# One decoder layer, two token halves in the MLP: accumulators opened by a copy, the scaled residual added later

## The chip, the cores and the metric

The kernel runs on one core of a Trainium2 chip. A core has a matrix engine (TensorE, PE in the profile), three engines for elementwise work (VectorE or DVE, ScalarE or ACT, GpSimd or POOL) and SyncE (SP), which here does nothing but issue transfers. Each engine runs its own instructions in order and waits on semaphores for the others. The metric is device time in microseconds, as the median of several executions. Tables and rows of the profile are from one further execution, recorded by the hardware profiler.

## The reference, cut to what matters

One decoder layer is computed for 2048 prompt tokens and for 32 decode tokens (8 sequences of 4). The first part (modulated input, a Mamba-2 group beside sliding-window attention, output projection, first layer norm) is not touched. The change lies in what follows:

```python
x = layer_norm(ALPHA * x + g_m * mixed, ln1_g, ln1_b)
h = x * (1.0 + sc_f) + sh_f
u = jnp.square(jax.nn.relu(jnp.einsum('btd,df->btf', h, w_up)))     # 1024 -> 4096
f = jnp.einsum('btf,fd->btd', u, w_down)                            # 4096 -> 1024
x = layer_norm(ALPHA * x + g_f * f, ln2_g, ln2_b)
```

The sum `ALPHA * x + g_f * f` is the subject. The kernel keeps the normalised but not yet scaled x of the prompt in DRAM as `xhat1_d`, so `ALPHA * x` is `xhat * ag1 + ab1`, with `ag1 = ALPHA * ln1_g` and `ab1 = ALPHA * ln1_b` as rows repeated over the partitions. The factor g_f is folded into the down-projection weights (`gf`).

## The kernel before, in words

The MLP is lines 1191 to 1494. It runs in two halves of eight tiles of 128 tokens. Half 1 has two column groups of 512 tokens in its up-projection, half 2 three of 352, since its last group also carries the 32 decode tokens.

The 4096 hidden features are 32 blocks of 128, called f. `up(f)` (L1242) makes one block for all tokens of the half: a group is 8 x 3 matmuls into a bank of PSUM named `sc`. There are three because each fp32 operand is split into a high and a low part (L161 to L168; weights `wuh`/`wul`, `wvh`/`wvl`, `wdh`/`wdl`). ACT then rectifies the group (L1254) and squares it into the high part (L1256), DVE squares it exactly (L1260) and POOL subtracts the two to get the low part (L1261). The pairs of high and low parts are named `x`/`ulx`, `u`/`B` and `A`/`ho` in turn. `ud` (L1259) is the decode tokens' part.

`down` (L1270) takes two blocks f and f+1 at a time: for each tile and each half of the 1024 columns six matmuls of 128x512 into a rotating bank (five of them: three named `mm`, two named `tr` in half 1 and `sc` in half 2), and then DVE adds the bank to the tile's accumulator (L1287). The accumulators are eight tiles of 128x1024 named `p`. In half 2 there are decode matmuls ahead of each (L1275). Sixteen pairs of blocks make up a half; one pair has two `up` and one `down`.

Weights come by SyncE's queue (L1128, 512 KB each) into one of three buffers `st`. Down-projection weights are scaled by DVE (L1137). ACT takes the high part of each (L162), POOL the low part (L163).

The accumulators begin as the scaled residual. `acc_load(t)` (L1224) loads xhat of a tile straight into `p` (L1226), `acc_init(t)` (L1228) multiplies by `ag1` and adds `ab1` in place (L1230, L1231, both DVE). For half 1 the loads are issued ahead of `up(1)` (L1406 to L1411). The initialisations go in a list `bg`, from which `slot()` (L1235) runs one entry after every group of an `up` and every tile of a `down`. For half 2 the entries of `bg` are filled at L1449: entry k has the layer norm of tile k of half 1 (`finish`: statistics L1320 and L1294, L173, L174, L1299 to a scale and shift, ACT L1303, DVE L1306, POOL L1307), the store of the tile before on ACT's queue (L1314), the load of half 2's accumulator two behind and its initialisation three behind. They run beside the last `down` of half 1 and the first `up` of half 2.

Program order is not the final order. A scheduler places each engine's instructions by its own model of their times, subject to what depends on what, so an edit in one place can move instructions in another.

Of the kernel before, what the change touches and what calls it, by code (L numbers as in the profile page):

```python
# [13 lines left out]
AF = mybir.ActivationFunctionType  # L14
ALU = mybir.AluOpType
# [104 lines left out]
def body(tc, I, O):  # L120
    nc = tc.nc
    V, S, G, PE, D = nc.vector, nc.scalar, nc.gpsimd, nc.tensor, nc.sync
# [3 lines left out]
    def pool(name, **kw):  # L126
        return tc.alloc_tile_pool(name=name, bufs=1, reuse_waits="tile", **kw)
# [3 lines left out]
    def mm_tile():  # L131
        return ps.tile([128, 512], F32, tag="mm", name="mm", bufs=3)

    def tr_tile():
        return ps.tile([128, 512], F32, tag="tr", name="tr", bufs=2)

    def sc_tile():
        return ps.tile([128, 512], F32, tag="sc", name="sc", bufs=3)

    xhat1_d = tc.dram_tile([NTOK, DM], F32, name="xhat1_d")  # L140
# [24 lines left out]
    def mm3(out, ahi, alo, bhi, blo, first=True, last=True):  # L165
        PE.matmul(out, lhsT=ahi, rhs=bhi, start=first, stop=False)  # L166
        PE.matmul(out, lhsT=ahi, rhs=blo, start=False, stop=False)  # L167
        PE.matmul(out, lhsT=alo, rhs=bhi, start=False, stop=last)  # L168
# [584 lines left out]
    for i in range(n + 3):  # L753
# [3 lines left out]
        t = g(i)  # L757
# [216 lines left out]
    def prt(i, dt_=F32):  # L974
        return pr.tile([128, 1024], dt_, tag=f"p{i}", name=f"p{i}")
# [47 lines left out]
    def ada_row(r, j, P):  # L1023
        if P == 128:
            return bcast(r, ada_d[0, 1024 * j:1024 * j + 1024])
        D.dma_start(out=r[:ND], in_=ada_d[1:9, 1024 * j:1024 * j + 1024].unsqueeze(1).to_broadcast([NB, NT_, 1024]))
        return r
# [98 lines left out]
    def wraw(nm, f, st=None):  # L1126
        st = st or t4("st")
        D.dma_start(out=st, in_=I["wu"][f].rearrange("p k n -> p (k n)") if nm == "wu" else I["wd"][f])  # L1128
        pre[nm, f] = st
# [11 lines left out]
    def wu_pq():  # L1141
        return [pq.tile([128, 1024], F32R, tag="wu" + c, name="wu" + c) for c in "hl"]
# [52 lines left out]
    def q4(tag):  # L1195
        nb, ty = T4[tag]
        return p4.tile([128, 512 if tag == "r" else 1024], ty, tag=tag, name=tag, bufs=nb)
# [3 lines left out]
    def t4(tag):  # L1201
        return f4.pop(tag) if tag in f4 else q4(tag)

    gf = t4("gf")
    fr = {nm: p4.tile([128, 1024], F32, tag=nm, name=nm) for nm in ("ag1", "ab1", "g2", "b2")}
# [10 lines left out]
    acc = {}  # L1216

    def rows_in():
        for nm, j in (("ag1", 2), ("ab1", 3)):
            bcast(fr[nm], I["rows"][j])  # L1220
        S.activation(fr["ag1"], fr["ag1"], AF.Copy, scale=ALPHA)
        S.activation(fr["ab1"], fr["ab1"], AF.Copy, scale=ALPHA)

    def acc_load(t):  # L1224
        a = acc[t] = prt((2, 3, 7, 4, 1, 5, 6, 0)[t % 8])
        D.dma_start(out=a, in_=xhat1_d[128 * t:128 * t + 128])  # L1226

    def acc_init(t):  # L1228
        a = acc[t]
        V.tensor_tensor(a, a, fr["ag1"], ALU.mult)  # L1230
        V.tensor_tensor(a, a, fr["ab1"], ALU.add)  # L1231

    bg = []

    def slot():  # L1235
        for fn in bg.pop(0) if bg else ():
            fn()

    def wup(f, eng=None):
        wu[f] = wtile("wu", f, *(wu_pq() if f % 2 == 0 else (t4("wvh"), t4("wvl"))), eng=eng)  # L1240

    def up(f, groups, H, u=None):  # L1242
        if f not in wu:
            wup(f)
        wh, wl, _ = wu.pop(f)
        uh, ul = u or u_pair()
        ud = None
        for j, (o, n) in enumerate(groups):
            mm = sc_tile()
            for k in range(8):  # L1250
                ks = slice(128 * k, 128 * k + 128)
                mm3(mm[:, :n], wh[:, ks], wl[:, ks], H[j][0][:, k, :n], H[j][1][:, k, :n], k == 0, k == 7)
            r = t4("r")
            S.activation(r[:, :n], mm[:, :n], AF.Relu)  # L1254
            w = min(n, 1024 - o)
            S.activation(uh[:, o:o + w], r[:, :w], AF.Square)  # L1256
            if w < n:
                ud = p4.tile([128, 32], F32, tag="ud", name="ud", bufs=4)
                V.tensor_tensor(ud, r[:, w:n], r[:, w:n], ALU.mult)  # L1259
            V.tensor_tensor(r[:, :w], r[:, :w], r[:, :w], ALU.mult)  # L1260
            G.tensor_tensor(ul[:, o:o + w], r[:, :w], uh[:, o:o + w].bitcast(F32), ALU.subtract)  # L1261
            slot()
        return uh, ul, ud
# [3 lines left out]
    def wdown(f):  # L1267
        return wtile("wd", f, t4("wdh"), t4("wdl"), gf)

    def down(us, ws, f0, t0, dec, after=None):  # L1270
        if dec is not None:
            for i, w in enumerate(ws):
                for n in range(2):
                    q = 32 * (2 * ((f0 + i) % 2) + n)
                    PE.matmul(dec[q:q + 32, :], lhsT=us[i][2], rhs=w[2][:, 512 * n:512 * n + 512],  # L1275
                              start=f0 + i < 2, stop=f0 + i >= 30, tile_position=(0, q))
        for j in range(8):
            t = t0 + j
            o = 128 * j
            for n in range(2):  # L1280
                sl = slice(512 * n, 512 * n + 512)
                mm = mm_tile() if dnc[0] % 5 < 3 else tr_tile() if dec is None else sc_tile()
                dnc[0] += 1
                for i, w in enumerate(ws):
                    mm3(mm, us[i][0][:, o:o + 128], us[i][1][:, o:o + 128], w[0][:, sl], w[1][:, sl], i == 0,
                        i == len(ws) - 1)
                V.tensor_tensor(acc[t][:, sl], mm, acc[t][:, sl], ALU.add)  # L1287
                if after:
                    after(j, n)
            slot()  # L1290
# [100 lines left out]
    for half in range(2):  # L1391
        t0 = 8 * half
        if half:
            groups, H = [(0, 352), (352, 352), (704, 352)], H3
            dec = tr_tile()
        else:
            groups, H = [(0, 512), (512, 512)], H2
        us, ws = {}, {}
        us[0] = up(0, groups, H)
        if not half:  # L1400
            wup(1, V)
            ada_row(gf, 5, 128)
        ws[0] = wdown(0)
        ws[1] = wdown(1)
        if not half:
            for j in range(2):  # L1406
                acc_load(j)
            rows_in()
            wraw("wu", 2)
            for j in range(2, 8):  # L1410
                acc_load(j)  # L1411
            ds = dec_steps()
            for j in range(8):
                bg.append([lambda j=j: acc_init(j)])
        us[1] = up(1, groups, H)
        for fb in range(15):
            f = 2 * fb
            us[f + 2] = up(f + 2, groups, H)
            if fb:
                ws[f] = wdown(f)  # L1420
                ws[f + 1] = wdown(f + 1)
            if half and fb == 14:
                ul31 = wu_pq()
                us[31] = up(31, groups, H, ul31)
                break
            down([us.pop(f), us.pop(f + 1)], [ws.pop(f), ws.pop(f + 1)], f, t0, dec)
            us[f + 3] = up(f + 3, groups, H)
            next(ds, None)
        if half:
            break  # L1430
        ph.release()
        ph = pool("h2b", side="right")
        H3 = [[ph.tile([128, 8, 352], F32R, name=f"H3_{j}{i}") for i in range(2)] for j in range(3)]
        ws[30] = wdown(30)
        ws[31] = wdown(31)
        wup(0)
        for j in range(3):
            for i in range(2):
                a = 352 * j
                while a < 352 * (j + 1):  # L1440
                    e = min((a // 128 + 1) * 128, 352 * (j + 1))
                    D.dma_start(out=H3[j][i][:, :, a - 352 * j:e - 352 * j].bitcast(F32),
                                in_=h2_d[a // 128][:, i, :, a % 128:a % 128 + e - a])
                    a = e
        wup(1)
        wraw("wd", 0)
        wraw("wd", 1)
        wraw("wu", 2)
        for sl_ in range(12):  # L1449
            todo = []  # L1450
            for lag, fn in ((0, lambda j: finish(j)), (1, lambda j: y_store(j, acc[j], 128, S)),
                            (2, lambda j: acc_load(8 + j)), (3, lambda j: acc_init(8 + j))):
                if 0 <= sl_ - lag < 8:
                    todo.append(lambda fn=fn, j=sl_ - lag: fn(j))
            bg.append(todo)
        down([us.pop(30), us.pop(31)], [ws.pop(30), ws.pop(31)], 30, t0, dec)

    ws[30] = wdown(30)
# [64 lines left out]
```

## Time and profile before

| | |
|---|---|
| median of 3 executions | 2485.43 us (2485.16 to 2487.25) |
| profiled execution | 2483.86 us |
| its span, first to last instruction | 2482.0 us |
| mean granted TensorE clock | 0.988 |
| DMA | 242.11 MB, mean 98 GB/s |
| L1230, all 16 | 1205 ns the shortest, 1212 the median, 3418 the longest |

In the rows of the profile L12 is line 12 of the kernel. A row of a timeline has the start, the duration, the engine, the line, the operation, `out<-in` by the program's names, the shape, and how many of the kind follow each other; in brackets how long the engine stood idle before it and what ended the wait. A row of the waits has who waited, for whom, the total in us, how often, and the longest. A row of groups has the count, the busy time with the mean duration in ns, and the idle time before it. Matmuls overlap, so one that takes 0.39 us starts 0.23 us after the one before it.

### The profile page before, as it was taken

The numbers are of one execution on the slowest core, as the hardware profiler recorded it, in microseconds if no ns is written. First come the engines' busy times: TensorE is split into PE (matmuls) and PEld (weight loads), VectorE is DVE, ScalarE is ACT, GpSimd is POOL, SyncE is SP. The second block draws the span as 40 slices with busy tenths as digits, with TensorE's granted clock in tenths as the row PEclk, the third lists the DMA queues.
The fourth block names the chain that finished last, engine by engine and source line by source line (L and its number), as shares of the span: only waits on it lengthen the run. The fifth ranks groups of instructions, "written<-read, shape, count | busy, mean of one in ns | idle before, by whom it ended". The sixth has DMA issues, their size and how long they took to land.

```text
span 2482.0 us, 32262 instructions
## 1 busy us (share of the span) xinstructions
PE 2407.5 (97%) x12695; PEld 2000.0 (81%) x12695; DVE 1466.3 (59%) x2549; ACT 764.0 (31%) x1546; POOL 883.4 (36%) x587
## 2 busy tenths in 40 slices
PE   7899999999999999899999999999999999999997
PEld 6567777987997888787888888887888888888885
DVE  6756665977788776845444344448744354354347
ACT  3544465432444545221211212112212212212221
POOL 4323430233233222642433424337422332332335
PEclk9999999999999999999999999999999999999998
DMA  8654242223315348221111211119210111111111
GB/s 317 255 186 163 89 157 84 73 67 120 98 62 190 128 161 285 90 66 56 59 43 43 64 43 54 49 37 267 74 52 34 43 60 34 43 60 35 43 47 70
DMA packets 116104, 242.11 MB, mean 98 GB/s; under 512 B 26080, under 2 KB 61360, under 8 KB 112800
## 3 DMA queue, kind: packets, MB, share of 16 engines
q1 hardware_dynamic: 111552, 230.07, 27.6%
q10 hardware_dynamic: 4400, 9.98, 1.0%
q8 instruction: 100, 1.64, 0.3%
q14 instruction: 52, 0.43, 0.1%
HBM read 185.66 MB, written 55.37 MB: 97 GB/s over the span
## 4 chain that ended last, share of the span: by engine, by line
PE 82%; DVE 10%; issue 3%; ACT 2%; POOL 2%; DMA 1%; POOLq 0%; DVEq 0%; SPq 0%; ACTq 0%
PE mm L166 12%; PE mm L168 12%; PE mm L167 12%; PE sc L166 11%; PE sc L167 11%; PE sc L168 11%; PE tr L166 2%; PE tr L168 2%; PE tr L167 2%; PE sc L462 1%; DVE xc L653 1%; PE mm L258 1%; DVE p L1230 1%; DVE csb L858 1%; PE tr L1275 1%
## 5 line engine op out<-in xcount | busy, mean ns | idle before, releaser
L163 POOL TENSOR_TENSOR wdl<-st,wdh 128x1024 fp32r<-128x1024 f32 x63 | 151.6, 2406 | 537.7 <-ACT wdh L162 537.6
L1260 DVE TENSOR_TENSOR r<-r 128x320 f32<-128x320 f32 (+1 forms) x160 | 146.4, 915 | 298.0 <-ACT u L1256 104.7
L1287 DVE TENSOR_TENSOR p<-mm,p 128x512 f32<-128x512 f32 x298 | 202.5, 687 | 175.2 <-PE mm L168 175.2
L162 ACT ACTIVATE wdh<-st 128x1024 fp32r<-128x1024 f32 x63 | 66.8, 1061 | 646.8 <-PE mm L168 263.3
L166 PE MATMUL sc<-H,wvh 128*128 128x352 f32 (+1 forms) x640 | 225.5, 352 | 5.5 <-ACT r L1254 5.5
L167 PE MATMUL sc<-H,wvh 128*128 128x352 f32 (+1 forms) x640 | 225.9, 353 | 0.0
L168 PE MATMUL sc<-H,wvl 128*128 128x352 f32 (+1 forms) x640 | 225.5, 352 | 0.0
L166 PE MATMUL sc<-H,wuh 128*128 128x352 f32 (+1 forms) x640 | 223.8, 350 | 0.0
L168 PE MATMUL sc<-H,wul 128*128 128x352 f32 (+1 forms) x640 | 223.1, 349 | 0.0
L167 PE MATMUL sc<-H,wuh 128*128 128x352 f32 (+1 forms) x640 | 222.8, 348 | 0.0
L1254 ACT ACTIVATE r<-sc 128x352 f32<-128x352 f32 (+1 forms) x160 | 81.5, 510 | 263.9 <-PE sc L168 225.9
L166 PEld LDWEIGHTS sc<-H,wvh 128*128 128x128 f32 x640 | 120.6, 188 | 18.2 <-ACT r L1254 5.9
L167 PEld LDWEIGHTS sc<-H,wvh 128*128 128x128 f32 x640 | 120.6, 188 | 12.3
L168 PEld LDWEIGHTS sc<-H,wvl 128*128 128x128 f32 x640 | 120.5, 188 | 12.1
L166 PEld LDWEIGHTS sc<-H,wuh 128*128 128x128 f32 x640 | 120.1, 188 | 11.1 <-ACT r L1254 0.8
L168 PEld LDWEIGHTS sc<-H,wul 128*128 128x128 f32 x640 | 120.4, 188 | 10.3
L167 PEld LDWEIGHTS sc<-H,wuh 128*128 128x128 f32 x640 | 120.3, 188 | 10.1
L174 POOL TENSOR_TENSOR rs<-ve,mhalf 128x1 f32<-128x1 f32 (+2 forms) x68 | 48.5, 714 | 207.5 <-DVE ve L173 182.7
L1137 DVE TENSOR_TENSOR st<-st,gf 128x1024 f32<-128x1024 f32 x64 | 86.6, 1353 | 50.6 <-POOL wdl L163 42.4
L1259 DVE TENSOR_TENSOR ud<-r 128x32 f32<-128x32 f32 x32 | 58.4, 1825 | 93.8 <-ACT r L1254 93.8
L1287 DVE TENSOR_TENSOR p<-tr,p 128x512 f32<-128x512 f32 x102 | 69.9, 687 | 73.8 <-PE tr L168 73.6
L1261 POOL TENSOR_TENSOR ulx<-r,x 128x512 fp32r<-128x512 f32 (+2 forms) x52 | 76.6, 1475 | 83.5 <-DVE r L1260 83.5
(485 smaller groups left out, 6608.9 us busy)
## 6 DMA issues: line engine op xcount, KB each, us to landing
st<-in_wd SPq DMA_DIRECT2D x64, 512.0 KB
st<-in_wu SPq DMA_DIRECT2D x63, 512.0 KB
wa<-in_w_ada SPq DMA_DIRECT2D x32, 512.0 KB
hT_d<-hb SPq DMA_DIRECT2D x16, 1024.0 KB
hT<-hT_d SPq DMA_DIRECT2D x16, 512.0 KB
hT<-hT_d SPq DMA_DIRECT2D x8, 1024.0 KB
csb<-cs_d SPq DMA_DIRECT2D x16, 512.0 KB
p<-xhat_d SPq DMA_DIRECT2D x16, 512.0 KB
```

Source lines behind the costliest of these rows:

```text
L162: S.activation(hi, src, AF.Copy)
L163: (eng or V).tensor_tensor(lo, src, hi.bitcast(F32), ALU.subtract)
L166: PE.matmul(out, lhsT=ahi, rhs=bhi, start=first, stop=False)
L167: PE.matmul(out, lhsT=ahi, rhs=blo, start=False, stop=False)
L168: PE.matmul(out, lhsT=alo, rhs=bhi, start=False, stop=last)
L174: G.tensor_tensor(r[:P], v[:P], mhalf[:P, 0:n], ALU.pow)
L1137: V.tensor_tensor(st, raw, scale, ALU.mult)
L1254: S.activation(r[:, :n], mm[:, :n], AF.Relu)
L1259: V.tensor_tensor(ud, r[:, w:n], r[:, w:n], ALU.mult)
L1260: V.tensor_tensor(r[:, :w], r[:, :w], r[:, :w], ALU.mult)
L1261: G.tensor_tensor(ul[:, o:o + w], r[:, :w], uh[:, o:o + w].bitcast(F32), ALU.subtract)
L1287: V.tensor_tensor(acc[t][:, sl], mm, acc[t][:, sl], ALU.add)
```

## The change

An accumulator is no longer loaded. `acc_open` only takes its tile. The first `down` of a half (`f0 == 0`) writes each bank into it by a copy on ACT; the later ones add as before. The scaled residual of a tile is made in a buffer of the `st` kind (the ones that weights come through) and added by one more DVE operation (`acc_res`). `residuals` puts one of these in the list of slots every 12 (half 1) or 14 (half 2) entries, after 14 or 16 empty ones, so that there is about one per pair of blocks.

```diff
-    def acc_load(t):
-        a = acc[t] = prt((2, 3, 7, 4, 1, 5, 6, 0)[t % 8])
-        D.dma_start(out=a, in_=xhat1_d[128 * t:128 * t + 128])
-
-    def acc_init(t):
-        a = acc[t]
-        V.tensor_tensor(a, a, fr["ag1"], ALU.mult)
-        V.tensor_tensor(a, a, fr["ab1"], ALU.add)
+    def acc_open(t):
+        acc[t] = prt((2, 3, 7, 4, 1, 5, 6, 0)[t % 8])
+
+    def acc_res(t):
+        r = t4("st")
+        D.dma_start(out=r, in_=xhat1_d[128 * t:128 * t + 128])
+        V.tensor_tensor(r, r, fr["ag1"], ALU.mult)
+        V.tensor_tensor(r, r, fr["ab1"], ALU.add)
+        V.tensor_tensor(acc[t], acc[t], r, ALU.add)
+
+    def residuals(t0, gap, step):
+        for _ in range(gap):
+            bg.append([])
+        for j in range(8):
+            bg.append([lambda j=j: acc_res(t0 + j)])
+            for _ in range(step - 1):
+                bg.append([])
...
-                V.tensor_tensor(acc[t][:, sl], mm, acc[t][:, sl], ALU.add)
+                if f0 == 0:
+                    S.activation(acc[t][:, sl], mm, AF.Copy)
+                else:
+                    V.tensor_tensor(acc[t][:, sl], mm, acc[t][:, sl], ALU.add)
...
-            for j in range(2):
-                acc_load(j)
+            for j in range(8):
+                acc_open(j)
             rows_in()
             wraw("wu", 2)
-            for j in range(2, 8):
-                acc_load(j)
             ds = dec_steps()
-            for j in range(8):
-                bg.append([lambda j=j: acc_init(j)])
+            residuals(0, 14, 12)
...
-        for sl_ in range(12):
+        for sl_ in range(10):
             todo = []
             for lag, fn in ((0, lambda j: finish(j)), (1, lambda j: y_store(j, acc[j], 128, S)),
-                            (2, lambda j: acc_load(8 + j)), (3, lambda j: acc_init(8 + j))):
+                            (2, lambda j: acc_open(8 + j))):
                 if 0 <= sl_ - lag < 8:
                     todo.append(lambda fn=fn, j=sl_ - lag: fn(j))
             bg.append(todo)
+        residuals(8, 16, 14)
```

Lines below the edit move by 9 to 12: L1254 becomes L1263, L1256 L1265, L1259 L1268, L1260 L1269, L1261 L1270, L1275 L1284, L1287 L1299 (and the new copy is L1297), L1306 L1318. In the new kernel L1229 is the residual's load, L1230 and L1231 work in its buffer and L1232 adds it.

The order of DVE's instructions where half 1 begins, before (`r` is the rectified group, `gf` the weights' scale):

```order
L1260 TENSOR_TENSOR r<-r 128x512
L1137 TENSOR_TENSOR st_9920<-st,gf 128x1024
L1230 TENSOR_TENSOR p_10009<-p_10009,ag_9927 128x1024
...
L1230 TENSOR_TENSOR p_10029<-p_10029,ag_9927 128x1024
L1137 TENSOR_TENSOR st_10005<-st,gf 128x1024
L1260 TENSOR_TENSOR r<-r 128x512
L1346 TENSOR_SCALAR g_9929<-g_9929,mean_all 32x1024
L1231 TENSOR_TENSOR p_10009<-p_10009,ab_9928 128x1024
```

The same place on DVE in the new kernel:

```order
L1269 TENSOR_TENSOR r<-r 128x512
L1137 TENSOR_TENSOR st_9920<-st,gf 128x1024
L1137 TENSOR_TENSOR st_10005<-st,gf 128x1024
L1269 TENSOR_TENSOR r<-r 128x512
L1358 TENSOR_SCALAR g_9929<-g_9929,mean_all 32x1024
L1360 SCALAR_TENSOR_TENSOR g_9929<-g_9929,b_9930 32x1024
L1269 TENSOR_TENSOR r<-r 128x512
L1363 SCALAR_TENSOR_TENSOR g_9929<-b_9930,g_9929 32x1024
L1269 TENSOR_TENSOR r<-r 128x512
L1230 TENSOR_TENSOR st<-st,ag_9927 128x1024
L1231 TENSOR_TENSOR st<-st,ab_9928 128x1024
```

Six multiplications that stood between the scaling of the first and of the second weight block are gone, and one residual follows after the squares.

DVE at the passage from half 1 to half 2, before (`p_145..` to `p_147..` are half 2's accumulators, `ud` the decode part):

```order
L1260 TENSOR_TENSOR r<-r 128x352
L1230 TENSOR_TENSOR p_14676<-p_14676,ag_9927 128x1024
L1287 TENSOR_TENSOR p_14503<-mm,p_14503 128x512 x2
L1231 TENSOR_TENSOR p_14676<-p_14676,ab_9928 128x1024
L1230 TENSOR_TENSOR p_14714<-p_14714,ag_9927 128x1024
L1259 TENSOR_TENSOR ud<-r 128x32
L1260 TENSOR_TENSOR r<-r 128x320
L1287 TENSOR_TENSOR p_14536<-sc,p_14536 128x512
L1230 TENSOR_TENSOR p_14748<-p_14748,ag_9927 128x1024
```

And in the new kernel:

```order
L1268 TENSOR_TENSOR ud<-r 128x32
L1269 TENSOR_TENSOR r<-r 128x320
L1230 TENSOR_TENSOR st<-st,ag_9927 128x1024
L1231 TENSOR_TENSOR st<-st,ab_9928 128x1024
L1269 TENSOR_TENSOR r<-r 128x352 x2
L1268 TENSOR_TENSOR ud<-r 128x32
L1232 TENSOR_TENSOR p_14519<-p_14519,st 128x1024
L1269 TENSOR_TENSOR r<-r 128x320
L1137 TENSOR_TENSOR st_15323<-st,gf 128x1024
L1137 TENSOR_TENSOR st_15331<-st,gf 128x1024
```

The accumulations of the first down-projection have left DVE for ACT, and one residual stands where there were eight initialisations.

SyncE's queue in the middle of half 1 of the new kernel, buffers numbered (`in_wd` and `in_wu` are weights):

```order
L1229 DMA st_10676<-xhat1_d_60 128x1024
L1128 DMA st_10713<-in_wd 128x1024
L1128 DMA st_10721<-in_wd 128x1024
L1128 DMA st_10857<-in_wu 128x1024
L1128 DMA st_10938<-in_wu 128x1024
L1229 DMA st_10974<-xhat1_d_60 128x1024
```

Where before there were the four weight loads of a pair of blocks, there is now a load of xhat ahead of each four, in the same rotation of three buffers.

## The prediction

> **What bounds the kernel now.** I read the page first (who is busy, and when), then the waits of TensorE, then the windows in which it waits, then the timelines there.
>
> ```profile
> PE 2407.5 (97%) x12695; PEld 2000.0 (81%) x12695; DVE 1466.3 (59%) x2549; ACT 764.0 (31%) x1546; POOL 883.4 (36%) x587
> PEclk9999999999999999999999999999999999999998
> ```
>
> TensorE (PE) is busy 97% of the span, at nearly full clock, so no edit of another engine's work can bring more than the few places where PE stands still. The change touches only the MLP, the last three fifths of the span. These are the waits of PE from 990 to 1800 us, which holds the start of the first token half, its middle, and the passage to the second half:
>
> ```profile
> PE sc L166 <- ACT r L1254: 5.5, 1, 5.5
> PE mm L168 <- POOL B L1261: 4.2, 1, 4.2
> PE mm L167 <- POOL wdl L163: 3.2, 1, 3.2
> PE mm L166 <- DVE p L1287: 2.0, 2, 1.8
> PE tr L1275 <- DVE ud L1259: 1.8, 1, 1.8
> ```
>
> Six waits, 16.7 us in 810 (that the sum below comes to the same figure is chance). The windows (start:end, length, then busy us of PE, PEld, DVE, ACT and POOL, the granted clock, DMA share, GB/s) put them in two places:
>
> ```profile
> 1010.00:1020.00 10.00, 5.21 (x21) 3.62 (x19) 7.47 (x6) 1.23 (x2) 10.00 (x3) 0.87 0.00 0
> 1020.00:1030.00 10.00, 7.43 (x22) 5.93 (x23) 9.69 (x5) 4.24 (x6) 9.91 (x6) 0.61 0.37 118
> 1720.00:1730.00 10.00, 4.54 (x21) 3.96 (x20) 8.07 (x7) 4.46 (x7) 8.84 (x5) 0.87 0.74 256
> 1760.00:1770.00 10.00, 9.74 (x34) 6.84 (x34) 10.00 (x13) 1.06 (x1) 3.28 (x2) 0.83 0.24 80
> 1100.00:1650.00 550.00, 550.00 (x2384) 445.46 (x2383) 242.83 (x284) 113.72 (x154) 196.06 (x102) 1.00 0.17 52
> 1800.00:2350.00 550.00, 550.00 (x2928) 487.61 (x2927) 242.43 (x309) 112.97 (x186) 176.86 (x117) 1.00 0.13 45
> ```
>
> The last two rows are the middles of the halves: PE never pauses, the clock is 1.00, and DVE, ACT and POOL are 44%, 21% and 36% (or less) busy. The other rows are the ramps: POOL and DVE full, PE waiting, the clock low after the wait. A matmul of 128x512 takes 550/2384 = 0.231 us from start to start in the middle; that is the yardstick below.
>
> **Term 1: the start of the first half.** PE there, then POOL, then DVE:
>
> ```profile
> 1014.03 0.39 PE L168 MATMUL sc<-H,wul 128*128 128x512 f32 x1
> 1017.61 0.80 PE L167 MATMUL mm<-wdl,u 128*128 128x512 f32 x1 [3.19 <-POOL wdl L163]
> 1022.57 0.80 PE L168 MATMUL mm<-wdh,B 128*128 128x512 f32 x1 [4.16 <-POOL B L1261]
> ...
> 1028.04 0.39 PE L166 MATMUL tr<-wdh,u 128*128 128x512 f32 x1
> ```
>
> ```profile
> 985.92 1.29 POOL L1261 TENSOR_TENSOR ulx<-r,x 128x512 fp32r<-128x512 f32 x1 [9.68 <-DVE r L1260]
> ...
> 1002.66 12.59 POOL L1261 TENSOR_TENSOR ulx<-r,x 128x512 fp32r<-128x512 f32 x1 [2.90 <-DVE r L1260]
> 1015.22 2.34 POOL L163 TENSOR_TENSOR wdl<-st,wdh 128x1024 fp32r<-128x1024 f32 x1
> ```
>
> ```profile
> 990.37 10.47 DVE L1230 TENSOR_TENSOR p<-p,ag 128x1024 f32<-128x1024 f32 x6 [2.08 <-DMA ab<-in_rows]
> ...
> 1003.23 5.75 DVE L1231 TENSOR_TENSOR p<-p,ab 128x1024 f32<-128x1024 f32 x5
> ...
> 1010.64 1.21 DVE L1230 TENSOR_TENSOR p<-p,ag 128x1024 f32<-128x1024 f32 x1
> ```
>
> One POOL subtraction that takes 1.29 us at 986 takes 12.59 us while DVE runs the accumulator initialisations (L1230, L1231) almost without a break. The weight split behind it (L163) is late for PE by 3.19 us, and the activation split B, behind that, by 4.16. The matmuls after them run slow. From 1014.03 to 1028.04 PE starts 15 recorded matmuls (the first of them counted, the last not): 14.01 - 15 x 0.231 = 10.5 us lost. The change takes fourteen of the sixteen operations of L1230/L1231 out of this stretch; one residual's pair stays near it. What is late next? The POOL subtraction would end at 1002.66 + 1.29 = 1003.95 and the split 2.34 later, at 1006.3, 8 us before PE asks for it at 1014.4. The chain to B (rectify, square, multiply, subtract) starts when POOL lets the buffer go at 1004 instead of 1015.2, so it comes 11 us earlier against a wait of 4.2. I take all 10.5. The bounds are 7.35, the two waits alone, and 10.5.
>
> The Trainium skill, "GPSIMD Engine Reference", section "Specifications", says that GpSimd shares its SBUF interfaces with VectorE and that VectorE instructions with two SBUF inputs contend for them. The 12.59 us row agrees. The rule speaks against the change too, since it adds a third such operation for each tile; that is the slower rival below.
>
> **Term 2: the passage to the second half.** Here the same initialisations stand in DVE's queue ahead of L1287, which empties the accumulation banks, and of L1259, which feeds the decode matmul:
>
> ```profile
> 1753.20 0.40 PE L168 MATMUL sc<-wdh,ulx 128*128 128x512 f32 x1
> 1755.38 0.51 PE L166 MATMUL mm<-wdh,A 128*128 128x512 f32 x1 [1.78 <-DVE p L1287]
> ...
> 1758.04 0.40 PE L168 MATMUL mm<-wdh,ulx 128*128 128x512 f32 x1
> 1760.26 1.05 PE L1275 MATMUL tr<-st,ud 128*32 128x512 f32 x4 [1.82 <-DVE ud L1259]
> 1761.26 0.51 PE L166 MATMUL sc<-wdh,A 128*128 128x512 f32 x1
> ...
> 1764.98 0.42 PE L166 MATMUL sc<-wdh,x 128*128 128x512 f32 x1
> ...
> 1770.28 0.50 PE L166 MATMUL mm<-wdh,A 128*128 128x512 f32 x1 [0.26 <-DVE p L1287]
> ```
>
> ```profile
> 1751.31 3.42 DVE L1230 TENSOR_TENSOR p<-p,ag 128x1024 f32<-128x1024 f32 x1
> 1754.65 1.28 DVE L1287 TENSOR_TENSOR p<-mm,p 128x512 f32<-128x512 f32 x2
> 1755.85 3.12 DVE L1231 TENSOR_TENSOR p<-p,ab 128x1024 f32<-128x1024 f32 x1
> ```
>
> The bank that PE wants at 1753.4 is emptied only after a 3.42 us multiplication. Lost: 1755.38 - 1753.20 - 0.23 = 1.95; 1760.26 - 1758.04 - 0.23 = 1.99; the nine steps from 1761.26 to 1764.98 take 3.72 instead of 9 x 0.231 = 2.08, so 1.64. The first matmul after each wait on L1287 runs slow too (0.51 and 0.50 instead of 0.40, so some 0.1 each), and the second such wait, at 1770, has 0.26 and a late start beside it, 0.4 in all: together 1.95 + 1.99 + 1.64 + 0.6 = 6.2 us. With the change the first down-projection leaves its banks through ACT and DVE has one residual there instead of eight initialisations, so all of it should go.
>
> The Trainium skill, "TensorE: Matmul & The Clock Gate", section "Part 1: The HAM clock gate", has the clock fall only after an idle window of about 3.4 us. Both waits here are shorter (1.78 and 1.82), and yet the steps after the second are slow (the 0.83 window). By the rule the 1.64 would not come from these waits and would stay, the sum would be 15.1 and the time 2470.3; I go by the rows.
>
> **What stays.** The largest wait, 5.5 us on L1254 at 1722 to 1728, is ACT's queue behind the layer norm of the first half (finish). Up to the end of that chain the order of DVE, POOL and ACT is unchanged, so I count nothing there.
>
> **What is added in the middles.** Each of 16 residuals brings three DVE operations of 128x1024 at 1.21 us (the 1010.64 row), 3.63 us; per half 29 us, of which 8 are additions that did not exist. Against that 16 of L1287 leave DVE per half for ACT:
>
> ```profile
> L1287 DVE TENSOR_TENSOR p<-mm,p 128x512 f32<-128x512 f32 x117 | 80.0, 689 | 93.9 <-PE mm L168 93.9
> L1254 ACT ACTIVATE r<-sc 128x512 f32<-128x512 f32 x51 | 30.0, 587 | 53.0 <-PE sc L168 53.0
> 1434.97 0.69 DVE L1287 TENSOR_TENSOR p<-mm,p 128x512 f32<-128x512 f32 x1 [0.69 <-PE mm L168]
> 1436.36 0.69 DVE L1287 TENSOR_TENSOR p<-mm,p 128x512 f32<-128x512 f32 x1 [0.69 <-PE mm L168]
> SPq L1128 <- DMA st<-in_wd: 82.2, 27, 4.0
> ```
>
> The nearest row for the ACT copy out of PSUM is L1254, the same shape: 0.59 us, against a bank every 1.39 us (1434.97 to 1436.36). ACT keeps up. Behind a copy wait the next rectify and the weight split, which then lag at most a copy or two.
>
> On DVE, a residual in a down-projection puts it 3.63 us behind; it regains 0.70 per bank. PE can run ahead by the five banks that rotate there, 5 x 1.39 = 6.9 us, so nothing reaches PE. The new wait is for the residual's own transfer: L1230 waits at the head of DVE's queue for xhat, and L1287 and L1260 behind it. The waits of SyncE's queue show a 512 KB load holding up the next by 4.0 us at the longest. Load and work in a row would make 7.6, 0.7 more than the banks cover: at worst 16 x 0.7 = 11 us. A gain in the middles is excluded, since PE is full there. Between 0 and 11 I take 0, because the transfers stand in SyncE's queue about a pair of blocks ahead and DMA is 17% busy.
>
> The 16 loads also move past weight loads on SyncE's queue and hold one of three `st` buffers until L1232. A weight needs its buffer for load and split, 4.0 + 1.2 + 2.4 = 7.6 us; four per pair of blocks through two buffers are 15 us of the 44 that a pair takes (96 matmuls of its down-projection and 2 x 48 of two up-projections, 192 x 0.231 = 44.4). Counted at nothing; without that cover one late weight costs some 3 us, as the 3.19 wait did.
>
> **The sum.** 10.5 + 6.2 = 16.7 us off the profiled execution of 2483.86 (span 2482.0): 2467.2. The median, 2485.43, lies 1.57 higher, so 2468.7, 0.7% faster. About 0.2%, 5 us, is what a measurement of this kernel can tell from no change.
>
> **Rivals.**
> (a) Only one ramp is mended, because another wait takes its place: the copies held in ACT's queue behind a weight split at 1750, or a split still late at 1014. For it: ACT is in order, and its copies stand among splits. Against it: the 8 us of margin. Time 2485.4 - 10.5 = 2474.9 or 2485.4 - 6.2 = 2479.2. Chance 0.13.
> (b) The other side: residuals cost in the middles what the initialisations cost in the ramps, by holding POOL off its splits. Sixteen operations cost PE 10.5 us at the first ramp, 0.66 each; 48 of them make 31.5, and the time 2485.4 - 16.7 + 31.5 = 2500.2. It is slower from 16.7/16 = 1.04 us per residual on. Against it:
>
> ```profile
> 1410.17 2.22 POOL L1261 TENSOR_TENSOR B<-r,u 128x512 fp32r<-128x512 f32 x1 [0.63 <-DVE r L1260]
> 1424.82 0.40 PE L168 MATMUL tr<-wdh,B 128*128 128x512 f32 x1
> ```
>
> in the middle B is done at 1412.4 and first used at 1424.8, 12 us later, and a residual's pair of operations lasts 2.4 us, not 16. Chance 0.05.
> (c) The 5.5 us wait at 1722 goes as well, since the eight xhat loads no longer run beside the layer norm's stores: 2463.2. The wait is for DVE and POOL steps, not for a transfer. Chance 0.07.
> (d) The change does not do what it says: the scheduler draws the residuals back into the ramps, and the time stays about 2485. The order shows one residual in each ramp, not eight. Chance 0.05.
>
> **How the numbers follow.** The forecast has the remaining 0.70. Range: from (c) with the slow steps after its wait, 2462, up to forecast plus the 11 us bound, 2480, which takes in (a). It leaves out (b) and (d), 0.10. Faster by over 0.2%: 0.70 + 0.13 + 0.07 = 0.90; within 0.2%: (d), 0.05; slower: (b), 0.05.
>
> **What would show it.** Right: no PE wait on POOL's wdl or B after 1000 us and none on L1299 or ud at the passage; the subtraction after L1269 back at 1.3 us; the 10-us windows there at PE 10.0 and clock 1.00; the 5.5 us wait still there; the middles still 100%. Wrong: PE waits in the middles on L1232, L1299, wdl or a split activation, once per pair of blocks (b, or the transfer bound); a wait on ACT's L1297 at either ramp (a).

## The result, and the profile after

The changed kernel takes 2467.2 us (median of 4, 2466.32 to 2468.51) against 2485.42 before: a ratio of 0.9926, 95% interval [0.9908, 0.9943]. Forecast was 2468.7. The kernel run once more beside later experiments (e10) gave 2469.03, ratio 0.9934 [0.9921, 0.9948]. That is the median of four executions; a fifth, of 3949 us at a granted clock of 0.556, was in a slow state and is left out. So the gain is 16 to 18 us, known to about 2 us.

The profiled execution has a span of 2465.2 us, 16.8 less than before. Its engines, and the waits of PE from the first MLP matmul to the end:

```profile
PE 2401.8 (97%) x12695; PEld 1997.0 (81%) x12695; DVE 1458.2 (59%) x2533; ACT 783.7 (32%) x1578; POOL 857.9 (35%) x587
```

```profile
PE sc L166 <- ACT r L1263: 5.0, 1, 5.0
PE mm L166 <- DVE p L1299: 0.6, 1, 0.6
```

Of the six waits before, one is left, the layer norm's, and one of 0.6 us is new. The windows at the start of half 1, at the passage, and in the middles:

```profile
1010.00:1020.00 10.00, 10.00 (x45) 8.19 (x45) 5.81 (x6) 5.44 (x8) 3.47 (x2) 1.00 0.42 131
1020.00:1030.00 10.00, 10.00 (x45) 8.13 (x44) 2.45 (x2) 4.39 (x8) 4.17 (x3) 1.00 0.26 90
1160.00:1170.00 10.00, 9.39 (x40) 7.06 (x39) 8.29 (x11) 0.00 (x0) 0.00 (x0) 1.00 0.25 79
1710.00:1720.00 10.00, 5.04 (x25) 4.47 (x24) 8.07 (x7) 4.78 (x7) 8.84 (x5) 0.89 0.33 129
1760.00:1770.00 10.00, 10.00 (x64) 10.00 (x63) 1.05 (x2) 2.63 (x5) 3.05 (x3) 1.00 0.01 2
1100.00:1650.00 550.00, 549.39 (x2378) 444.34 (x2377) 270.89 (x305) 110.92 (x149) 188.71 (x100) 1.00 0.18 58
1800.00:2350.00 550.00, 550.00 (x2943) 487.84 (x2942) 264.36 (x324) 117.57 (x192) 181.58 (x120) 1.00 0.16 52
```

At 1010 to 1030 PE is full at full clock. In the middles DVE is 22 to 28 us busier in 550, and PE is as full as it was but for the 0.6 us.

Two marks in PE's timeline cut the gain into pieces. These are the last matmul before the wait on the layer norm and the first one after it, before the change:

```profile
1722.08 0.40 PE L168 MATMUL mm<-wdh,ho 128*128 128x512 f32 x1
1727.93 0.66 PE L166 MATMUL sc<-H,wvh 128*128 128x352 f32 x1 [5.46 <-ACT r L1254]
```

And in the changed kernel:

```profile
1712.89 0.40 PE L168 MATMUL mm<-wdh,ho 128*128 128x512 f32 x1
1718.24 0.66 PE L166 MATMUL sc<-H,wvh 128*128 128x352 f32 x1 [4.96 <-ACT r L1263]
```

The first MLP matmul starts at 978.07 before and 978.38 after, the last at 2463.50 and 2446.71. So from the first matmul to the first mark half 1 takes 744.01 and 734.51: 9.50 us gained. The wait itself, 5.85 and 5.35: 0.50. From there to the last matmul, 735.57 and 728.47: 7.10. The MLP gains 17.1. What is ahead of it, in which nothing was changed, came out 0.3 longer, which leaves the 16.8 of the spans. That part differs from execution to execution: in the thirteen traces the first MLP matmul starts between 977.2 us (e11) and 982.1 us (e3), and in the two traces of the changed kernel at 978.38 and 979.68. The time from the first to the last MLP matmul is therefore the finer measure of a trace: 1485.4 us before, 1468.3 and 1468.8 in the changed kernel.

### The profile page after: what moved, and what is told of

It reads as the page before. It is cut to its first block, busy times and chain, and to the rows that moved or that the text cites. A ratio compares the mean times of both kernels' runs of the same rounds, so it can differ in the third digit from the quotient of the medians.

```text
span 2465.2 us, 32266 instructions
## 1 busy us (share of the span) xinstructions
PE 2401.8 (97%) x12695; PEld 1997.0 (81%) x12695; DVE 1458.2 (59%) x2533; ACT 783.7 (32%) x1578; POOL 857.9 (35%) x587
## 4 chain that ended last, share of the span: by engine, by line
PE 49%; DVE 2%; POOL 1%; issue 1%; ACT 0%; DMA 0%; POOLq 0%; DVEq 0%; ACTq 0%
PE sc L166 10%; PE sc L168 10%; PE sc L167 10%; PE mm L166 5%; PE mm L168 5%; PE mm L167 5%; PE tr L166 1%; PE tr L168 1%; PE tr L167 1%; PE tr L1284 1%; DVE p L1299 1%; DVE nb L1311 0%; DVE p L1318 0%; POOL rs L174 0%; DVE bst L1332 0%
## 5 line engine op out<-in xcount | busy, mean ns | idle before, releaser
L1269 DVE TENSOR_TENSOR r<-r 128x320 f32<-128x320 f32 (+1 forms) x160 | 131.1, 821 | 300.0 <-ACT A L1265 102.4
L1299 DVE TENSOR_TENSOR p<-mm,p 128x512 f32<-128x512 f32 x278 | 187.7, 685 | 123.2 <-PE mm L168 123.0
L1263 ACT ACTIVATE r<-sc 128x352 f32<-128x352 f32 (+1 forms) x160 | 81.6, 511 | 292.1 <-PE sc L168 281.9
L1137 DVE TENSOR_TENSOR st<-st,gf 128x1024 f32<-128x1024 f32 x64 | 112.6, 1759 | 95.4 <-POOL wdl L163 65.5
L653 DVE SCALAR_TENSOR_TENSOR xc<-xq,cvw,xc 128x256 f32<-128x256 f32 x192 | 102.2, 536 | 2.7
L1268 DVE TENSOR_TENSOR ud<-r 128x32 f32<-128x32 f32 x32 | 48.2, 1506 | 91.1 <-ACT r L1263 91.1
L163 POOL TENSOR_TENSOR wvl<-st,wvh 128x1024 fp32r<-128x1024 f32 x32 | 77.1, 2411 | 63.7 <-ACT wvh L162 60.7
```

Of the source, the lines that this page charges most:

```text
L163: (eng or V).tensor_tensor(lo, src, hi.bitcast(F32), ALU.subtract)
L653: V.scalar_tensor_tensor(dst_, src(j), cvw[:, f, j:j + 1], dst_, ALU.mult, ALU.add)
L1137: V.tensor_tensor(st, raw, scale, ALU.mult)
```

## The experiments

The theory has two parts. The gain is what PE lost in two ramps, where DVE's initialisations held up the first down-projection's inputs and banks. The work that moved costs nothing in the middles, because there PE is the bound and the others have room. The rivals: the parts need each other; the copies on ACT are what helps; every moved operation goes on costing PE a share.

**One half at a time.** In e1 only half 1 is changed, in e2 only half 2; the other half keeps the old loads and initialisations.

```diff
-                if f0 == 0:
+                if f0 == 0 and t0 == 0:      # e2: t0 == 8
...
-                            (2, lambda j: acc_open(8 + j))):
+                            (2, lambda j: acc_load(8 + j)), (3, lambda j: acc_init(8 + j))):
...
-        residuals(8, 16, 14)
```

> Half 1 as in the changed kernel, half 2 as before (loads into the accumulators, two operations on each beside the layer norm). Theory: the gain is two separate ramps, and the shift of the traces at the passage gives the first 9.5 us, so 2485.4 - 9.5 = 2475.9, within 1 us, with the waits on L1287's line and on ud at the passage back as they were (2.0 and 1.8 us). Rival, the two parts help each other (a shorter first half leaves the second other transfers to run beside): 2473 or less, or 2479 or more.

> Half 1 as before, half 2 as in the changed kernel. Theory: the passage alone, 16.8 - 9.5 = 7.3 us of the span by the traces, so 2478.1, within 1 us, with the waits on wdl (3.2 us) and B (4.2 us) at the start of half 1 back and one POOL subtraction near 12 us long. Rival, the parts help each other: e1 and e2 together save 2 us more or less than the 18.2 of the whole.

Measured: e1 2474.28 us, ratio 0.9957 [0.9944, 0.9969]; e2 2479.24, ratio 0.9974 [0.9965, 0.9983]; before beside them 2485.17. The waits of PE in the MLP in e1:

```profile
PE sc L166 <- ACT r L1272: 5.6, 1, 5.6
PE tr L1293 <- DVE ud L1277: 1.8, 1, 1.8
PE mm L166 <- DVE p L1308: 1.4, 2, 0.9
PE sc L166 <- DVE p L1308: 0.8, 2, 0.4
```

And in e2:

```profile
PE sc L166 <- ACT r L1272: 5.4, 1, 5.4
PE mm L168 <- POOL B L1279: 4.2, 1, 4.2
PE mm L167 <- POOL wdl L163: 2.6, 1, 2.6
```

Each has the waits of its unchanged half, e1 those on the banks in four pieces in place of two (2.1 us against 2.0), and POOL's long subtraction is back in e2 (12.61 us). The gains, 10.9 and 5.9, add up to 16.8, and the whole is 18.2 and 16.4 us in its two measurements. The parts do not need each other. e1 came 0.6 us below its range and e2 0.1 above.

**What the residuals cost in the middles.** e3 leaves them out, e8 makes and adds each twice.

```diff
-            residuals(0, 14, 12)
...
-        residuals(8, 16, 14)
```

```diff
-            bg.append([lambda j=j: acc_res(t0 + j)])
+            bg.append([lambda j=j: acc_res(t0 + j)] * 2)
```

> The changed kernel without its residuals: no xhat loads and none of L1230 to L1232; the outputs lack ALPHA * x in the MLP's sum. Theory: the 48 DVE operations and 16 loads cost nothing in the middles but one bank wait of 0.6 us, so 2466.5, within 1 us of the changed kernel. Rival, the residuals cost a part of what they cost in the ramps (0.35 us per operation or more) and the ramps gave that much more: 2467.2 - 48 x 0.35 = 2450, or between.

> The changed kernel with every residual made and added twice (the outputs have ALPHA * x twice). Theory: the middles have room, and 16 x 3.6 = 58 us more on DVE come to PE only where two residuals in a row, 7.3 us, pass the 6.9 us that five banks cover: 0 to 10 us more than the changed kernel, 2467 to 2477. Rival, each operation costs PE 0.35 us or more wherever it stands: 2467.2 + 48 x 0.35 = 2484 or more.

Measured: e3 2469.35, ratio 0.9937 [0.9923, 0.9950]; e8 2470.54, ratio 0.9939 [0.9923, 0.9954]. The middles of e8:

```profile
1100.00:1650.00 550.00, 550.00 (x2382) 445.24 (x2381) 282.82 (x323) 111.81 (x150) 196.83 (x101) 1.00 0.20 65
1800.00:2350.00 550.00, 550.00 (x2937) 487.04 (x2936) 277.74 (x342) 116.86 (x192) 183.33 (x120) 1.00 0.18 58
```

No residuals is no faster than one per pair: e3 is 0.3 to 2.2 us above the changed kernel's two medians. The forecast for it, 2466.5 within 1 us, missed. Its trace shows where: it does not have the bank wait of 0.6 us in half 1, but it has 18 groups of decode matmuls in place of 17 (last section), a layer norm's wait of 5.9 us and a new one of 0.5 us on a split activation, and its MLP takes 1470.3 us. Two residuals per pair is 1.5 to 3.3 us slower (MLP 1471.7). DVE is 50 to 51% busy in e8's middles, and PE still never stops there. A price of 0.35 us per operation is refuted from both sides: it would have made e3 2450 and e8 2484. e8's one new wait is 0.7 us in the first down-projection (PE on the copy, L1297).

**ACT or DVE for the copies.** e4 copies the first banks on DVE.

```diff
-                    S.activation(acc[t][:, sl], mm, AF.Copy)
+                    V.tensor_copy(acc[t][:, sl], mm)
```

> The changed kernel with the first down-projection's banks copied by DVE in place of ACT. Theory: what counts is that the initialisations are out of the ramps; 32 copies of at most 0.69 us on DVE against a bank every 1.39 us leave PE alone, so the same as the changed kernel, 2467 to 2469. Rival, taking the banks off DVE is part of the gain: the two ramps lose 2 to 4 us each again, 2471 to 2475.

Measured: 2470.68, ratio 0.9944 [0.9932, 0.9957], 1.7 to 3.5 us above the changed kernel's two medians, between what the theory and the rival gave. The waits of PE:

```profile
PE sc L166 <- ACT r L1263: 5.5, 1, 5.5
PE mm L166 <- DVE p L1299: 0.7, 1, 0.7
PE tr L166 <- DVE p L1299: 0.4, 1, 0.4
```

Neither ramp is back (no wait on wdl, B or ud); the 0.7 and 0.4 are at 1160 us, in the middle of half 1. By the medians 14.5 of some 17 us come without ACT. The MLP of this trace takes 1472.9 us, 4.1 to 4.6 more than in the changed kernel. Most of that is found at other places than the copies: two more groups of decode matmuls (2.1 us), eight more slow steps behind the layer norm's wait (1.1) and the larger bank waits (0.6). Whether the copies on DVE are why the scheduler grouped the decode matmuls otherwise, and so whether ACT gives the remaining 2 to 3 us, is not settled.

**Why the ramps lose: DVE's queue, or POOL kept from SBUF.** e5 is the kernel before, with each accumulator's two operations replaced by four statistics of one input.

```diff
-        V.tensor_tensor(a, a, fr["ag1"], ALU.mult)
-        V.tensor_tensor(a, a, fr["ab1"], ALU.add)
+        for i in range(4):
+            o = 512 * (i % 2)
+            V.bn_stats(junk, a[:, o:o + 512])
```

> The kernel before, with the two operations on each accumulator (two inputs from SBUF, 1.21 us each) replaced by four statistics of 128x512 (one input, 0.67 us each); the residual goes in unscaled. DVE's load in the ramps is the same or a little more (2.7 us a tile against 2.4). Theory: the operations cost PE time because they keep POOL from SBUF, so without a second input POOL's subtraction takes 1.3 to 3 us in place of 12.6, the waits on wdl and B go, and the time is 2470 to 2477. Rival: it is DVE's queue, in which the squares and the scaling of weights stand behind them; then the ramps lose the same, 2484 to 2488.

Measured: 2470.61, ratio 0.9942 [0.9927, 0.9958]. The first ramp from 990 to 1030 us, before:

```profile
990.00:1030.00 40.00, 32.65 (x129) 25.73 (x128) 36.79 (x25) 12.17 (x17) 31.57 (x10) 0.87 0.37 129
```

The same in e5, with POOL's B operations and the DVE rows beside the first of them:

```profile
990.00:1030.00 40.00, 40.00 (x174) 32.46 (x173) 35.98 (x46) 11.91 (x17) 22.30 (x11) 1.00 0.48 162
```

```profile
1002.11 1.29 POOL L1263 TENSOR_TENSOR B<-r,u 128x512 fp32r<-128x512 f32 x1
...
1007.40 1.61 POOL L1263 TENSOR_TENSOR B<-r,u 128x512 fp32r<-128x512 f32 x1 [0.62 <-DVE r L1262]
```

```profile
999.81 3.60 DVE L1232 BATCH_NORM_STATS2 junk<-p 128x6 f32<-128x512 f32 x5
```

DVE is as full, 36.0 of 40 us against 36.8, but POOL's operation beside five statistics in a row takes 1.29 us where it took 12.59 beside a row of L1231, and PE never waits. So DVE being busy is not what held POOL up; a row of the multiplications and additions was. They differ from the statistics in a second input from SBUF and in an output of 1024 numbers per partition in place of 6, and this run does not separate the two. It took a row, too: beside single ones of these operations, at 1020 to 1030 us, POOL's subtractions in the kernel before took 2.2 to 2.3 us. One more thing is not isolated: the scheduler started the statistics earlier and set the second weight block's scaling ahead of more of them, so a share of e5's gain may be order.

**Where the residuals stand.** e7 puts a half's eight in eight slots running, e11 puts them as early as they can be, right behind the first down-projection's copies.

```diff
-            residuals(0, 14, 12)
+            residuals(0, 60, 1)     # e11: residuals(0, 4, 1)
...
-        residuals(8, 16, 14)
+        residuals(8, 70, 1)         # e11: residuals(8, 7, 1)
```

> The changed kernel with a half's eight residuals in eight slots running, from about a third of the half on, in place of one per pair of blocks. Theory: out of the ramps is not enough, the spread matters, because the eight loads stand ahead of weight loads in SyncE's queue and in the three buffers, and 8 x 3.6 = 29 us of DVE fall in a stretch: PE waits 4 to 15 us in each half, 2475 to 2497. Rival: out of the ramps is enough, 2467 to 2469.

> The changed kernel with all eight residuals of a half as early as they can stand, right behind the copies of the first down-projection, one per tile. Theory: the initialisations cost time by standing ahead of what the first down-projection needs; behind it they can only hold up the second pair's weights (eight loads of 512 KB ahead of them, 24 operations of 1.2 us on DVE), so the waits on wdl and B before the first one stay away and PE loses 2 to 12 us in each half, 2471 to 2491, on a weight split or a bank. Rival 1, two-input operations near the ramp cost 0.66 us each as before: 2467 + 48 x 0.66 = 2499. Rival 2, once the first down-projection has its inputs nothing is lost: 2467 to 2469.

Measured: e7 2477.8, ratio 0.9971 [0.9960, 0.9983]; e11 2486.62, ratio 1.0006 [0.9997, 1.0015]: the whole gain is gone. PE's waits in e7:

```profile
PE sc L166 <- ACT r L1263: 5.4, 1, 5.4
PE mm L166 <- DVE p L1299: 2.7, 2, 1.6
PE mm L166 <- ACT wdh L162: 1.8, 1, 1.8
PE mm L167 <- POOL wdl L163: 0.8, 1, 0.8
```

In e11, and behind them, for the first half, the issues on SyncE's queue, what that queue waited for from 1000 to 1080 us, and PE:

```profile
PE sc L166 <- ACT wvh L162: 10.1, 2, 5.6
PE sc L166 <- ACT r L1263: 5.4, 1, 5.4
PE sc L168 <- POOL wvl L163: 0.7, 2, 0.4
PE sc L168 <- POOL wul L163: 0.5, 1, 0.5
```

```profile
1011.98 18.77 SPq L1229 DMA_DIRECT2D st<-xhat_d  x5
1033.98 3.74 SPq L1128 DMA_DIRECT2D st<-in_wu  x2
```

```profile
SPq L1229 <- DVE p L1232: 21.7, 5, 8.9
```

```profile
1038.45 0.79 PE L166 MATMUL sc<-H,wvh 128*128 128x512 f32 x1 [4.50 <-ACT wvh L162]
```

In e11 the waits on wdl and B stay away, as the theory had it, and a new one takes their place. Five loads of xhat go out one by one from 1012 to 1031 us, as each `st` buffer is handed on by the residual in it. The next two up-projection weights stand behind them until 1034, and PE waits 4.5 us for a split. For some 6 us behind that wait the matmuls start mostly 0.42 us apart in place of 0.23 (the granted clock from 1040 to 1050 us is 0.77). Counted matmul by matmul from the first one of the MLP, e11 is 9.4 us ahead of the kernel before in front of that wait and 1.5 behind these slow steps: 8 us lost for a wait of 4.5. Half 2 loses 8 us more in the same way (5.6 us of wait). e7 shows the milder form: 2.7 us on banks in half 1 and 2.6 on late weight splits in half 2, under the 4 to 15 us of waits in each half that were expected. The time was within its range because late starts behind the waits and three more groups of decode matmuls (20 in place of 17) came on top. So what the change brings needs both: the copy takes the initialisations from ahead of the first down-projection, and the spread keeps three buffers, one queue and DVE free. Which of these three counts most was not tried one by one.

**The wait that is left.** e6 is the changed kernel with the layer norm's last addition on DVE; e9 also starts half 1's residuals later.

```diff
     def finish(t):
...
-        ln_out(a, 128, st)
+        ln_b(a, 128, *ln_a(128, st))
+        ln_c(a, 128, V)
...
-            residuals(0, 14, 12)
+            residuals(0, 86, 12)    # e9 only
```

> The changed kernel with the last addition of half 1's layer norm (L1319, 128x1024, 2.4 us each on POOL) on DVE. Theory: the 5.0 us wait that is left at the passage is POOL's queue, where the reciprocal roots stand behind these additions; eight of them off POOL are 19 us, DVE has room for 8 x 1.21 = 9.7 since the initialisations left, and the wait with the 1.4 us of slow steps behind it goes: 2460.5 to 2463. Rival: the wait is the length of the chain over the engines, or DVE becomes late in its place: 2466 to 2470.

> e6 (layer norm's last addition on DVE) and half 1's residuals begun after 86 empty slots in place of 14, when the decode rows' steps are over. Theory: the loss of 1.3 to 1.7 us at 1160 us is a residual beside those steps on DVE, so it goes: 2459.5 to 2461, and no PE wait from 990 to 1690 us. Rival, it is the residual or the decode step alone: the wait stays or moves to another pair, 2461 to 2463.

> The changed kernel once more, word for word, beside the two others of this call, since experiments that keep the ramps free ended 2 to 3 us apart. Theory: 2466 to 2469, with one bank wait of 0.6 us in the middle of half 1 and about 5 us on the layer norm's queue at the passage. Rival, those 2 to 3 us are only the scatter from one execution to the next: then this one ends as often near 2470.

Measured: e6 2461.65, ratio 0.9904 [0.9888, 0.9919]; e9 2460.41, ratio 0.9898 [0.9883, 0.9913]; the changed kernel again (e10) 2469.03, with waits of 5.5 and 0.6. That is at the upper end of e10's forecast and 1.8 us above the first median of the same kernel, so two kernels whose medians are 2 us apart can't be told apart by them. The layer norm's addition and the small step L1311 behind the reciprocal root in the changed kernel, and then in e6:

```profile
L1319 POOL TENSOR_TENSOR p<-p,b 128x1024 f32<-128x1024 f32 x8 | 20.3, 2536 | 3.7 <-DVE p L1318 3.7
L1311 DVE SCALAR_TENSOR_TENSOR nb<-mvf,rs 128x1 f32<-128x1 f32 x8 | 7.4, 931 | 0.4 <-POOL rs L174 0.4
```

```profile
L1319 DVE TENSOR_TENSOR p<-p,b 128x1024 f32<-128x1024 f32 x8 | 10.4, 1294 | 0.0
L1311 DVE SCALAR_TENSOR_TENSOR nb<-mvf,rs 128x1 f32<-128x1 f32 x8 | 1.9, 232 | 0.3 <-POOL rs L174 0.3
```

20.3 us leave POOL, 10.4 come to DVE, and PE no longer waits at the passage: a gain of 5.6 us against the changed kernel's first median, 7.4 against the second. About 1 us of it is not this wait: e6 has 16 groups of decode matmuls, the changed kernel 17. DVE's small steps between POOL's are shorter as well (0.93 us each, then 0.23), so the wait hung on POOL's additions, but not only by their length in POOL's queue: how much each part gave is not separated. In e9 PE stands still nowhere from 1000 to 2400 us:

```profile
1000.00:2400.00 1400.00, 1400.00 (x6805) 1189.90 (x6805) 680.09 (x818) 319.60 (x479) 489.04 (x293) 1.00 0.20 63
```

The wait at 1165 us is gone, as it is in e3 without residuals, so it takes the residuals beside the decode rows' steps on DVE. DVE there in the changed kernel:

```profile
1163.53 1.21 DVE L1386 SCALAR_TENSOR_TENSOR g<-b,g 32x1024 f32<-32x1024 f32 x1 [1.71 <-DMA b<-ada_d]
1164.67 1.27 DVE L1299 TENSOR_TENSOR p<-mm,p 128x512 f32<-128x512 f32 x2
```

The addition that PE needs stands behind a decode step that itself waits for a transfer. It depends on how they meet: e8, with two residuals in place of one, has no PE wait there. The 1.2 us between e6 and e9 is too little to be told from nothing by the times alone. e9 beats both kernels.

## Why the prediction was right, point by point

**Term 1, 10.5 us.** Counted matmul by matmul, the changed kernel is 10.6 us ahead when the first ramp is over. From the first matmul to the passage 9.5 of it is left, since the new bank wait at 1165 us with its late starts took 1.1. PE has no gap from 990 to 1030. e1, which has this part alone, gained 10.9. The margins held: POOL's subtractions there took 1.3 to 2.3 us instead of 12.59.

**Term 2, 6.2 us.** Measured behind the wait: 7.1. By the same count 6.1 of it falls at the passage, and the last microsecond is not in the term: the decode matmuls came in 17 groups in place of 18, 18.9 us busy against 20.0. e2, which has this part alone, gained 5.9. The slow steps went with the two waits of 1.8 us: the window at 1760 to 1770 is at 1.00 now, where it was at 0.83. The forecast had taken it so against the Trainium skill ("TensorE: Matmul & The Clock Gate", section "Part 1: The HAM clock gate"), which has the clock go down after an idle window of about 3.4 us. In e1 the wait of 1.82 us on ud is back, behind one of 0.92, and no slow steps follow: the windows from 1745 to 1765 are at 1.00. What shorter waits must add up to before the clock falls stays open.

**What stays.** The layer norm's wait did, 4.96 and 5.5 us in two executions. e6 shows what it hung on: the additions on POOL.

**The middles at nothing.** Off by the one wait of 0.6 us, 1.1 with its late starts. The sum had set the residual alone against five banks; the decode rows' steps on DVE, which stand in the same place and wait for transfers (e9), were not in it. e3 and e8 bear out the zero elsewhere.

**The sum.** That 16.7 was forecast and 17.1 measured in the traces is in part luck: 1.1 us lost at 1165 us stands against 0.5 from a shorter layer norm's wait and 1.0 from the grouping of decode matmuls, and none of the three was forecast.

**The rivals.** (b), residuals that cost everywhere, is refuted by e3 and e8; its argument, that these operations on DVE hold POOL off its splits, is right for the ramp (e5); in the middle, with POOL's results 12 us early, it costs nothing. (a) and (d) did not happen. (c) did not either: the eight loads left, the wait stayed. The bound from the residual's load, 11 us, was not reached. e7 and e11 show that this rests on the spread: with the residuals close together the buffers and the queue do not cover them.

## What to carry to other kernels

Where one engine is the bound almost everywhere, add up its waits by place; what moves work out of such a place gains that place's loss and no more. Moved work is free only if its loads and buffers are spread as well as its operations: the same residuals gained 17 us at one per pair of weight blocks, 7 in a clump, and nothing directly behind the ramp. And elementwise work on one engine can make a third one late: look at how long a known operation of that engine takes beside other work (1.29 us or 12.59 here), not only at who is busy.

## What the runs showed of the hardware that was not expected

A group of decode matmuls (32 columns of weights, `tr<-st,ud`) costs about the same with four as with eight in it. The first row is of the changed kernel, the second of the kernel before, the third of the changed kernel:

```profile
1723.92 1.05 PE L1284 MATMUL tr<-st,ud 128*32 128x512 f32 x4
```

```profile
2030.21 1.06 PE L1275 MATMUL tr<-st,ud 128*32 128x512 f32 x8
```

```profile
2397.09 1.91 PE L1284 MATMUL tr<-st,ud 128*32 128x512 f32 x12
```

Inside the group of eight, four start within 0.02 us of each other and the next four 0.45 us later. The kernel writes the two matmuls of a block into strips of 32 columns, four strips for a pair of blocks; in a group of four only two start together. So how the scheduler groups them is worth 1 us a group: 18 groups in the kernel before, 19 in e4, 17 in the changed kernel, 16 in e6, always 128 recorded matmuls. None of these edits meant to touch that.

After the layer norm's wait PE's clock stayed low for a time that differs from trace to trace with nearly the same wait: some 10 slow steps of 128x352 (0.29 us in place of 0.16) after 5.46 us in the kernel before, 18 after 5.54 us in e4. That is 8 x 0.13, some 1.1 us more. Why it differs was not tried. With the groups it is a good part of the differences between the MLPs of kernels with free ramps, such as e4's. It does not explain the two medians of the changed kernel: both its traces have 17 groups and 10 slow steps, and the medians are 1.8 us apart.
